# Row maxima from half-array matmuls in batches of four banks, in a two-layer encoder on one NeuronCore

## The chip, the core and the metric

The kernel runs on one core of one Trainium2 chip. A core has a matrix engine (TensorE, in the profile PE for its matmuls and PEld for its weight loads), a vector engine (DVE), a scalar engine (ACT), a general engine (POOL), an engine that only issues transfers (SP), and 16 DMA engines. Matmul results land in PSUM, which has eight banks of 128 partitions by 512 float32 numbers; everything else lies in SBUF. The engines run side by side, each working through its own list of instructions in order, and wait for each other through semaphores. The metric is the device time of one execution in microseconds (us), as the median of several runs.

## The reference

Two layers; in each, a normalised input is projected, one group of columns goes through a gated mixer and another through attention, and an output projection follows. The change touches attention alone:

```python
def gqa_axial_attention(q, k, v, qn_g, kn_g, tables):
    q = rmsnorm(q.reshape(b, s, H_B, HEAD_DIM), qn_g)
    k = rmsnorm(k.reshape(b, s, KV_HEADS, HEAD_DIM), kn_g)
    q = apply_axial_rope(q, tables)
    k = apply_axial_rope(k, tables)
    ...
    def attend(qblk):
        sc = jnp.einsum('bqkgd,bskd->bkgqs', qblk, k).astype(jnp.float32) * scale
        p = jax.nn.softmax(sc, axis=-1).astype(v.dtype)
        return jnp.einsum('bkgqs,bskd->bqkgd', p, v)
...
    y = jnp.concatenate([y_a, y_b], axis=-1)
    out = jnp.einsum('bse,ed->bsd', y, w_out[l])
    x = x + rmsnorm(out, post_g[l])
```

There are 2048 tokens, 8 query heads that share 2 key/value heads, and a head size of 64. A softmax needs a number near the largest score of each query row, which is subtracted before the exponential so that nothing overflows; any number near it gives the same softmax.

## The kernel before, in words

**Precision.** The operands are kept as two float16 parts, a high half and a low half. A product of two such operands takes three matmul passes.

**Layers and phases.** Each layer runs a projection phase (`Project.run`, matmul groups `pp`) and then an attention phase (`attend`). Work that isn't on the main line of a phase is hung into it at fixed places: `Background` (`bg`) runs jobs at ticks of the projection, one tick each 8 matmuls of 256 columns or each 4 of 512; in attention, `at(k, f)` hangs a job `f` at key tile `k`.

**Units and key tiles.** A unit is one tile of 128 tokens with one key/value head, four query heads wide, so there are 32 units in a layer. A unit goes over 16 key tiles (`NT`), and the main loop of `attend` counts key tiles of all units: `k = 16 u + n`, 512 in a layer. At each key tile PE makes a score bank `sp` with two matmuls of 512 columns, ACT reads it twice (`p_hi`, the exponential in float16, and `p_f`, the same in float32), and POOL or DVE makes the low half of it, `p_lo = p_f - p_hi`. Three key tiles later (`LAG`) PE takes twelve short matmuls of these against the values, into the bank `po`, which lives through the unit.

**Row maxima.** The maximum of a row must be known before its unit begins, so maxima are worked out ahead: for a unit, 4 heads times 4 groups of 512 keys make 16 steps. One step (`max_step`) is a matmul of 512 columns into a bank `pmax` and a reduction of it by DVE into a column of `mx`. The weights are `q_m`, in which partitions 0 to 63 hold the high half of the queries and 64 to 127 the low half, and `k_st` holds the high half of the keys twice, one copy in each half of the partitions. So a full-array matmul over 128 partitions gives high plus low half of the queries against the high half of the keys. The first 7 units (`PRE`) of a layer have their maxima in the projection phase, one step at each tick; the other 25 in the attention phase, spread evenly over its key tiles (`span`), 0.78 of a step at each. After the 16 steps `max_row` and `stack_max` (a transpose `t2` and two short rows) put the negated maxima into memory, from where the unit loads them as a part of `q2`.

**Filling work.** The output projection of a tile (48 matmuls `pout` of 512 columns, `out_steps`) is put into the list `fill`; at each key tile `pop_fill` takes some of them, spread evenly up to the key tile `fill_to` by `weight(k)`.

**End of a unit.** `gate` and `mul` (`finish`) read the bank `po` two key tiles after the last products; `turn_at` then transposes the tile's result (`py`), and `more` adds its output products to `fill`.

**What sets the order.** In attention all engines keep the program's order (`Pinned`). Within a key tile PE has: the two `sp` matmuls; the jobs hung there, `pmax` among them; the output products; and the twelve `po` matmuls of the key tile three back. All of `sp`, `pmax`, `pout`, `po`, `py`, `t2`, `pp` share the eight PSUM banks (`ps_t`). A new one takes the bank that was freed earliest in the program, and its first matmul waits until that bank's last reader is through.

**Who subtracts.** `dve_share(k)` gives 15 of 100 key tiles' `p_lo` to DVE and the others to POOL.

The helper `Pinned` records its engine's calls at line 89, so most instructions of attention carry the label L89 in the profile and are told apart by the names of their tiles.

Of the kernel before, what the change touches and what calls it, by code (L numbers as in the profile page):

```python
# [14 lines left out]
ALU = mybir.AluOpType  # L15
# [28 lines left out]
def encoder(ctx: ExitStack, tc, x, w_in, w_out, pre_g, post_g, ln_a_g, ln_a_b,  # L44
# [31 lines left out]
    def ps_t(name):  # L76
        return psum.tile([P, GRP], F32, name=name, tag="ps", bufs=8)
# [818 lines left out]
    Q_DELAY = 16  # L896
    PRE = 7
    PRE_WAIT = 19
    SHARE_0 = 15
    SHARE = 15  # L900
    T_DELAY = 9
    VA_DELAY = 13
    LAG = 3
# [8 lines left out]
    def attend(l, kv, nxt):  # L912
# [27 lines left out]
        def at(k, f):  # L940
            later.setdefault(k, []).append(f)
# [4 lines left out]
        def load_hl(dst, u):  # L946
            t, kv = units[u]
            for a in range(2):
                nc.sync.dma_start(dst[a * HD:(a + 1) * HD], q_d[t // TPG][kv, a, t % TPG])

        def load_qm(u):
            s = state[u]
            s.qm = f_t("q_m", dt=F16)
            load_hl(s.qm, u)
            s.mx = small.tile([P, NQ, NG], F32, name="mx", bufs=3)

        def load_q(u):
# [5 lines left out]
            nc.sync.dma_start(s.q2[0:HD], q_d[t // TPG][kv, 0, t % TPG])  # L963
            nc.sync.dma_start(s.q2[HD:HD + 2], m_d[t][kv])

        def max_step(u, n, pe, dve):
            s = state[u]
            j, c = n // NG, n % NG
            kv = units[u][1]
            ps = ps_t("pmax")  # L970
            pe.matmul(ps, s.qm[:, j * P:(j + 1) * P], k_st[:, kv, c * GRP:(c + 1) * GRP], start=True, stop=True)
            dve.tensor_reduce(s.mx[:, j, c:c + 1], ps, AX.X, ALU.max)  # L972

        def max_row(u, dve):
            s = state[u]
            s.m = small.tile([P, NQ], F32, name="m_neg", bufs=3)
            dve.tensor_reduce(s.m, s.mx, AX.X, ALU.max, negate=True)
# [248 lines left out]

        pre = min(PRE, len(units) - 2)
        steps = NQ * NG
        span = ((len(units) - 1) * NT - 16) // (len(units) - pre)

        def before():

            n0 = 0
            for u in range(pre):
                bg.add(n0 - 10 + PRE_WAIT, lambda u=u: load_qm(u))
                for n in range(steps):
                    bg.add(n0 + 4 + n + PRE_WAIT, lambda u=u, n=n: max_step(u, n, PE, nc.vector))
                bg.add(n0 + steps + 6 + PRE_WAIT, lambda u=u: max_row(u, nc.vector))
                bg.add(n0 + steps + 10 + PRE_WAIT, lambda u=u: stack_max(u, PE, nc.scalar, nc.vector))
                n0 += steps  # L1240
            bg.add(n0 + 4 + PRE_WAIT, lambda: load_q(0))
            bg.add(n0 + 4 + PRE_WAIT, lambda: load_qm(pre))
# [29 lines left out]
        for u in range(1, len(units)):  # L1272
            at(u * NT - 10, lambda u=u: load_q(u))
        for u in range(pre, len(units)):
            k0 = (u - pre) * span
            if k0 >= 8:
                at(k0 - 8, lambda u=u: load_qm(u))
            for n in range(steps):
                at(k0 + n * span // steps, lambda u=u, n=n: max_step(u, n, PE, DVE))
            at(k0 + span + 1, lambda u=u: max_row(u, DVE))  # L1280
            at(k0 + span + 5, lambda u=u: stack_max(u, PE, ACT, DVE))

        def load_gb(t):
            tiles[t].gb = f_t("gb")
# [2 lines left out]
        def pop_fill(n):  # L1287
            for _ in range(n):
                if fill:
                    fill.pop(0)()  # L1290

        def weight(k):
            return 2 if k >= total - 2 * NT else 1

        end = total + LAG
# [3 lines left out]

        def dve_share(k):  # L1300

            n = SHARE_0 if k < NH * NT else SHARE
            return k * n // 100 != (k + 1) * n // 100

        W_EARLY = total - 5 * NT
        gb_pieces = []
# [25 lines left out]
        def turn_at(k, t, cs):  # L1332
            trans, split = turn_steps(t, cs)
            at(k, trans)
            at(k + 1, split)
# [8 lines left out]
        for k in range(end):  # L1344
            if k < total:
                u, i = k // NT, k % NT
                s = state[u]
                kv = units[u][1]
                if i == 0 and kv == 0:
                    load_gb(units[u][0])  # L1350
                ss = slice(i * P, (i + 1) * P)
                sp = ps_t("sp")
                PE.matmul(sp, k_st[:, kv, ss], s.qs, start=True, stop=False)
                PE.matmul(sp, k_lo[0:HD + 2, kv, ss], s.q2[0:HD + 2], start=False, stop=True)
                ACT.activation(p_hi(k), sp, AF.Exp)
                ACT.activation(p_f(k), sp, AF.Exp)
                if not dve_share(k):
                    sub_lo(k, POOL)
            if post_queue:
                post_queue.pop(0)()  # L1360
            kb = k - 1
            if 0 <= kb < total and dve_share(kb):
                sub_lo(kb, DVE)
            for f in later.pop(k, []):
                f()
            if fill:
                room = sum(weight(q) for q in range(k, max(k + 1, fill_to)))
                pop_fill(-(-len(fill) * weight(k) // room))
            kb = k - LAG
            if 0 <= kb < total:  # L1370
                u, i = kb // NT, kb % NT
                s = state[u]
                kv = units[u][1]
                if i == 0:
                    s.av = ps_t("po")[:, 0:NQ * (HD + 1)].rearrange("p (t e) -> p t e", e=HD + 1)
                v_hi, v_lo = v16[:, i, kv, HD:VN], v16[:, i, kv, 0:HD]
                for j in range(NQ):
                    lhs = p_hi(kb)[:, j * P:(j + 1) * P]
                    PE.matmul(s.av[:, j], lhs, v_hi, start=i == 0 and j == 0, stop=False, skip_group_check=True)
                    PE.matmul(s.av[:, j, 0:HD], lhs, v_lo, start=False, stop=False, skip_group_check=True)  # L1380
                for j in range(NQ):
                    lhs = p_lo(kb)[:, j * P:(j + 1) * P]
                    PE.matmul(s.av[:, j], lhs, v_hi, start=False, stop=i == NT - 1, skip_group_check=True)
                if i == NT - 1:
                    t = units[u][0]
                    gate, mul = finish(u)
                    if u + 1 == len(units):
                        break
                    at(k + 1, gate)
                    at(k + 2, mul)  # L1390
                    if t == NT - 1:
                        turn_at(k + 6, t, (0, 1))
                        if nxt is None:
                            at(end - 1, lambda: last.extend(last_first()))
                        else:
                            more(k + 8, last_first, end)
                    elif kv == 1:
                        turn_at(k + 6, t, range(4))
                        if t in held:
                            more(k + 8, lambda t=t: held_steps(t), end)  # L1400
                        else:
                            more(k + 8, lambda t=t: out_steps(t), min(k + 8 + 2 * NT, end))
        assert not later
        gate()
        mul()
# [136 lines left out]
```

## Time and profile before

| | |
|---|---|
| runs | 2459.73, 2459.85, 2460.52 us; median 2459.85 us |
| the profiled execution | 2460.9 us, of which its span (first to last instruction) 2459.1 us |
| granted TensorE clock in it | 0.997 |
| attention of layer 0 and of layer 1 | about 554 to 1237 us and 1766 to 2440 us |
| matmuls `pmax` | 1024 (224 in the projections, 800 in attention) |

The profile gives for each engine its busy time, and in its timeline the start of each instruction with its length. A matmul's length there is its passage through the array with a modelled end, and the next one starts before it is over; what a matmul takes of PE's time is the distance from its start to the next start.

### The profile page before, as it was taken

The numbers are of one execution on the slowest core, as the hardware profiler recorded it, in microseconds if no ns is written. First come the engines' busy times: TensorE is split into PE (matmuls) and PEld (weight loads), VectorE is DVE, ScalarE is ACT, GpSimd is POOL, SyncE is SP. The second block draws the span as 40 slices with busy tenths as digits, with TensorE's granted clock in tenths as the row PEclk, the third lists the DMA queues.
The fourth block names the chain that finished last, engine by engine and source line by source line (L and its number), as shares of the span: only waits on it lengthen the run. The fifth ranks groups of instructions, "written<-read, shape, count | busy, mean of one in ns | idle before, by whom it ended". The sixth has DMA issues, their size and how long they took to land. (4 is left out here: it accounts for less than half of the span.)

```text
span 2459.1 us, 62836 instructions
## 1 busy us (share of the span) xinstructions
PE 2415.6 (98%) x25327; PEld 1600.6 (65%) x25327; DVE 1743.1 (71%) x4001; ACT 1638.0 (67%) x3545; POOL 1190.1 (48%) x1000
## 2 busy tenths in 40 slices
PE   7999999999999999999999999999999999999997
PEld 6988776445666666666589987754456666666664
DVE  7678556867777777777676875688667767777774
ACT  6565223148888888888854742231688888888886
POOL 2210110037777777777721111100577777777776
PEclk9999999999999999999999999999999999999999
DMA  6352222222121212121243422221321111212120
GB/s 199 121 178 72 66 62 64 67 88 73 51 81 52 67 51 70 60 64 49 83 166 113 152 60 71 73 73 43 110 63 38 57 54 43 68 43 68 51 68 27
DMA packets 174916, 188.11 MB, mean 76 GB/s; under 512 B 19608, under 2 KB 143648, under 8 KB 174624
## 3 DMA queue, kind: packets, MB, share of 16 engines
q1 hardware_dynamic: 174192, 182.52, 24.5%
q8 instruction: 198, 3.24, 0.6%
q10 hardware_dynamic: 432, 1.57, 0.2%
q14 instruction: 94, 0.77, 0.1%
HBM read 129.38 MB, written 54.66 MB: 75 GB/s over the span
## 5 line engine op out<-in xcount | busy, mean ns | idle before, releaser
L89 POOL TENSOR_TENSOR p_parts<-p_f,p_parts 128x512 f16<-128x512 f32 x872 | 1032.6, 1195 | 334.3 <-ACT p_f L89 253.9
L89 ACT ACTIVATE p_parts<-sp 128x512 f16<-128x512 f32 x1024 | 619.3, 605 | 175.1 <-PE sp L89 126.5
L89 PEld LDWEIGHTS <-p_parts 128*128 128x128 f16 x12288 | 510.0, 97 | 250.4 <-POOL p_parts L89 6.2
L89 DVE TENSOR_REDUCE mx<-pmax 128x1 f32<-128x512 f32 x800 | 541.4, 683 | 177.5 <-PE pmax L89 174.2
L89 PE MATMUL pp<-w_hl,hT 128*128 128x256 f16 x5376 | 619.3, 274 | 3.6 <-ACT w_hl L89 3.4
L89 ACT ACTIVATE p_f<-sp 128x512 f32<-128x512 f32 x1024 | 617.7, 603 | 0.0
L89 PEld LDWEIGHTS <-hT 128*128 128x128 f16 x5376 | 526.1, 98 | 70.8 <-issue 3.4
L89 PE MATMUL po<-v_st,p_parts 128*128 128x65 f16 (+1 forms) x12288 | 542.7, 193 | 7.0 <-POOL p_parts L89 4.5
L89 PE MATMUL pout<-wo,y_t 128*128 128x512 f16 x1536 | 488.2, 378 | 1.9 <-ACT y_t L89 1.7
L89 PE MATMUL sp<-q,k_t 66*128 66x512 f16 x1024 | 390.5, 381 | 0.0
L89 PE MATMUL sp<-q_st,k_t 128*128 128x512 f16 x1024 | 388.3, 379 | 1.6 <-DVE o_tok L89 1.3
L89 PE MATMUL pmax<-k_t,q_m 128*128 128x512 f16 x1024 | 387.1, 379 | 0.5 <-DVE hT L89 0.3
L89 PE MATMUL pp<-hT,w_hl 128*128 128x512 f16 x1536 | 370.3, 379 | 0.0
L89 PEld LDWEIGHTS <-y_t 128*128 128x128 f16 x1536 | 148.8, 97 | 177.8 <-ACT y_t L89 3.4
L89 PEld LDWEIGHTS <-w_hl 128*128 128x128 f16 x1536 | 149.6, 98 | 174.0
L89 PEld LDWEIGHTS <-q_m 128*128 128x128 f16 x1024 | 101.1, 99 | 120.9 <-issue 0.3
L972 DVE TENSOR_REDUCE mx<-pmax 128x1 f32<-128x512 f32 x224 | 150.2, 685 | 37.1 <-PE pmax L89 36.9
L89 POOL TENSOR_TENSOR wo<-wo_raw,wo 128x512 f16<-128x512 f32 x32 | 37.0, 1157 | 264.3 <-PE pp L89 223.0
L89 DVE TENSOR_TENSOR p_parts<-p_f,p_parts 128x512 f16<-128x512 f32 x152 | 118.0, 776 | 37.4 <-ACT p_f L89 36.6
L629 POOL TENSOR_TENSOR fl<-fv,fh 128x512 f16<-128x512 f32 x32 | 37.9, 1203 | 209.0 <-ACT fh L628 200.3
L89 PEld LDWEIGHTS <-k_t 128*128 128x128 f16 (+1 forms) x2048 | 131.3, 98 | 3.8 <-DVE o_tok L89 1.4
L547 ACT ACTIVATE fc<-pp,rs_y 128x64 f32<-128x64 f32 x320 | 69.7, 355 | 71.6 <-DVE rs_y L124 71.6
(212 smaller groups left out, 2042.9 us busy)
## 6 DMA issues: line engine op xcount, KB each, us to landing
w_raw<-in_w_in_dram SPq DMA_DIRECT2D x20, 512.0 KB
w_raw<-in_w_in_dram SPq DMA_DIRECT2D x10, 1024.0 KB
gb_d<-fa SPq DMA_DIRECT2D x32, 256.0 KB
wo_row<-in_w_out_dram SPq DMA_DIRECT2D x16, 512.0 KB
wo_raw<-in_w_out_dram SPq DMA_DIRECT2D x16, 512.0 KB
z_d<-fb SPq DMA_DIRECT2D x32, 256.0 KB
fb<-z_d SPq DMA_DIRECT2D x32, 256.0 KB
ya_d<-fa SPq DMA_DIRECT2D x32, 256.0 KB
```

Of the source, the lines that this page charges most:

```text
L89: return tc.keep_in_program_order(call(*args, **kw))
L547: nc.scalar.activation(qn[:, t, h], src[:, t, h], AF.Copy, scale=rs[:, i, t, h:h + 1])
L629: nc.gpsimd.tensor_tensor(s.lo, vh, s.hi, ALU.subtract)
L972: dve.tensor_reduce(s.mx[:, j, c:c + 1], ps, AX.X, ALU.max)
```

## The change

Four things are changed in how row maxima are made and placed.

- `load_qm` loads the high half of the queries into both halves of `q_m`'s partitions (two transfers of the same size as before). The low half of the queries no longer enters the row maximum, so this number differs slightly from before.
- `max_step` becomes `max_batch`: one head at a time, its four key groups together. Four banks are taken, four matmuls follow, each over 64 partitions, alternately the lower and the upper half, and then four reductions by DVE. In the projection phase a batch stands at each fourth tick.
- In attention the batches stand at the key tiles 0, 5, 8 and 13 of a unit (`BATCH`, from key tile 5 of the phase and up to 22 before the last unit), 100 of them, evenly picked from these. `weight(k)` is 0 there, so no output products are taken in these key tiles.
- `dve_share` is now the key tiles 1 and 10 of each unit, 2 of 16. `mul` comes one key tile earlier, the transposes of a finished tile two later, its output products one later. The last tile keeps its places.

```diff
-    SHARE_0 = 15
-    SHARE = 15
+    SHARE = (1, 10)
+    BATCH = (0, 5, 8, 13)
+    BATCH_FIRST = 5
...
             s.qm = f_t("q_m", dt=F16)
-            load_hl(s.qm, u)
+            t, kv = units[u]
+            for a in range(2):
+                nc.sync.dma_start(s.qm[a * HD:(a + 1) * HD], q_d[t // TPG][kv, 0, t % TPG])
...
-        def max_step(u, n, pe, dve):
+        def max_batch(u, j, pe, dve):
             s = state[u]
-            j, c = n // NG, n % NG
             kv = units[u][1]
-            ps = ps_t("pmax")
-            pe.matmul(ps, s.qm[:, j * P:(j + 1) * P], k_st[:, kv, c * GRP:(c + 1) * GRP], start=True, stop=True)
-            dve.tensor_reduce(s.mx[:, j, c:c + 1], ps, AX.X, ALU.max)
+            pm = [ps_t("pmax") for _ in range(NG)]
+            for c in range(NG):
+                r = slice(c % 2 * HD, c % 2 * HD + HD)
+                pe.matmul(pm[c], s.qm[r, j * P:(j + 1) * P], k_st[r, kv, c * GRP:(c + 1) * GRP],
+                          start=True, stop=True)
+            for c in range(NG):
+                dve.tensor_reduce(s.mx[:, j, c:c + 1], pm[c], AX.X, ALU.max)
...
-        span = ((len(units) - 1) * NT - 16) // (len(units) - pre)
+        slots = [u * NT + n for u in range(len(units) - 1) for n in BATCH]
+        slots = [k for k in slots if BATCH_FIRST <= k < (len(units) - 1) * NT - 22]
+        wanted = (len(units) - pre) * NQ
+        assert len(slots) >= wanted
+        slots = [slots[n * len(slots) // wanted] for n in range(wanted)]
...
-                for n in range(steps):
-                    bg.add(n0 + 4 + n + PRE_WAIT, lambda u=u, n=n: max_step(u, n, PE, nc.vector))
+                for j in range(NQ):
+                    bg.add(n0 + 4 + NG * j + PRE_WAIT, lambda u=u, j=j: max_batch(u, j, PE, nc.vector))
...
-            for n in range(steps):
-                at(k0 + n * span // steps, lambda u=u, n=n: max_step(u, n, PE, DVE))
-            at(k0 + span + 1, lambda u=u: max_row(u, DVE))
-            at(k0 + span + 5, lambda u=u: stack_max(u, PE, ACT, DVE))
+            own = slots[(u - pre) * NQ:(u - pre + 1) * NQ]
+            if u > pre:
+                at(own[0] - 8, lambda u=u: load_qm(u))
+            for j, k in enumerate(own):
+                at(k, lambda u=u, j=j: max_batch(u, j, PE, DVE))
+            at(own[-1] + 2, lambda u=u: max_row(u, DVE))
+            at(own[-1] + 6, lambda u=u: stack_max(u, PE, ACT, DVE))
...
         def weight(k):
+            if k in slots:
+                return 0
             return 2 if k >= total - 2 * NT else 1
...
-            n = SHARE_0 if k < NH * NT else SHARE
-            return k * n // 100 != (k + 1) * n // 100
+            return k % NT in SHARE
...
-                    at(k + 2, mul)
+                    at(k + 1, mul)
...
-                        turn_at(k + 6, t, range(4))
+                        turn_at(k + 8, t, range(4))
```

How the order moves is shown at two places. The first is PE in the attention of layer 1: one key tile with a row maximum before, and one with a batch now. `LDWEIGHTS` is a weight load and names what is loaded; `q_31935` is the tile `q2`; a bracket names the engines whose semaphore the instruction waits for. Before:

```order
40239 L89 LDWEIGHTS k_t
40240 L89 MATMUL sp<-q_st,k_t 128x512 [waits DVE_49]
40241 L89 LDWEIGHTS k_t
40242 L89 MATMUL sp<-q_31935,k_t 128x512
40243 L89 LDWEIGHTS q_m [waits DMAHW1_49,DMAHW0_49]
40244 L89 MATMUL pmax<-k_t,q_m 128x512 [waits Activation_49]
40245 L89 LDWEIGHTS y_t
40246 L89 MATMUL pout<-wo,y_t 128x512
40247 L89 LDWEIGHTS p_parts
40248 L89 MATMUL po<-v_st,p_parts 128x65
```

Now:

```order
40366 L89 LDWEIGHTS k_t
40367 L89 MATMUL sp<-q_31935,k_t 128x512
40368 L89 LDWEIGHTS q_m
40369 L89 MATMUL pmax<-k_t,q_m 128x512 [waits DVE_49]
40370 L89 LDWEIGHTS q_m
40371 L89 MATMUL pmax<-k_t,q_m 128x512 [waits Activation_49]
40372 L89 LDWEIGHTS q_m
40373 L89 MATMUL pmax<-k_t,q_m 128x512 [waits DVE_49]
40374 L89 LDWEIGHTS q_m
40375 L89 MATMUL pmax<-k_t,q_m 128x512 [waits DVE_49]
```

Four `pmax` stand together where one stood with an output product; each waits for the reader of the bank that it takes over, DVE or ACT, and the twelve `po` matmuls and the next key tile's `sp` are queued behind them.

The second place is DVE in the attention of layer 0, around the end of a unit (`rden`, `gb` and `o_tok` are `gate` and `mul`). Before:

```order
1376 L89 TENSOR_REDUCE mx<-pmax 128x1 [waits PE_49]
1377 L89 TENSOR_SCALAR rden<-po,cols 128x4 [waits PE_49]
1378 L89 RECIPROCAL rden<-rden 128x4 [waits DVE_49]
1379 L89 TENSOR_TENSOR gb<-gb,rden 128x2x2x64 [waits DVE_49]
1380 L89 TENSOR_REDUCE mx<-pmax 128x1 [waits PE_49]
1381 L89 TENSOR_TENSOR o_tok<-po,gb 128x2x2x64 [waits DVE_49]
1382 L89 TENSOR_REDUCE mx<-pmax 128x1 [waits PE_49]
1383 L89 TENSOR_TENSOR p_parts<-p_f,p_parts 128x512 [waits Activation_49]
1384 L89 TENSOR_REDUCE mx<-pmax 128x1 [waits PE_49] x3
```

Now:

```order
1126 L89 TENSOR_TENSOR p_parts<-p_f,p_parts 128x512 [waits Activation_49]
1127 L89 TENSOR_REDUCE m_neg<-mx 128x4 [waits DVE_49]
1128 L89 TENSOR_SCALAR rden<-po,cols 128x4 [waits PE_49]
1129 L89 RECIPROCAL rden<-rden 128x4 [waits DVE_49]
1130 L89 TENSOR_TENSOR gb<-gb,rden 128x2x2x64 [waits DVE_49]
1131 L89 TENSOR_TENSOR o_tok<-po,gb 128x2x2x64 [waits DVE_49]
1132 L89 TENSOR_REDUCE mx<-pmax 128x1 [waits PE_49] x4
1133 L89 SCALAR_TENSOR_TENSOR m_rows<-t_12903,m_rows 4x128 [waits DMAHW2_49,Activation_49]
1134 L89 TENSOR_REDUCE mx<-pmax 128x1 [waits PE_49] x4
1135 L89 TENSOR_TENSOR o_t<-pout,g_post 128x512 [waits Activation_49]
```

The reductions stood singly between other work; now they come in fours, one batch right behind `gate` and `mul`, the next with hardly anything of DVE's between.

More of the change, by code (lines that the diff above doesn't have):

```diff
@@ L1274, in attend @@
         for u in range(pre, len(units)):
-            k0 = (u - pre) * span
-            if k0 >= 8:
-                at(k0 - 8, lambda u=u: load_qm(u))
-            for n in range(steps):
-                at(k0 + n * span // steps, lambda u=u, n=n: max_step(u, n, PE, DVE))
-            at(k0 + span + 1, lambda u=u: max_row(u, DVE))
-            at(k0 + span + 5, lambda u=u: stack_max(u, PE, ACT, DVE))
+            own = slots[(u - pre) * NQ:(u - pre + 1) * NQ]
[5 more added lines that the diff above has]
+            at(own[-1] + 6, lambda u=u: stack_max(u, PE, ACT, DVE))
         def load_gb(t):
@@ L1367, in attend @@
                 room = sum(weight(q) for q in range(k, max(k + 1, fill_to)))
-                pop_fill(-(-len(fill) * weight(k) // room))
+                pop_fill(-(-len(fill) * weight(k) // max(room, 1)))
             kb = k - LAG
@@ L1397, in attend @@
                     elif kv == 1:
-                        turn_at(k + 6, t, range(4))
+                        turn_at(k + 8, t, range(4))
                         if t in held:
-                            more(k + 8, lambda t=t: held_steps(t), end)
+                            more(k + 9, lambda t=t: held_steps(t), end)
                         else:
-                            more(k + 8, lambda t=t: out_steps(t), min(k + 8 + 2 * NT, end))
+                            more(k + 9, lambda t=t: out_steps(t), min(k + 9 + 2 * NT, end))
         assert not later
```

## The prediction

> **What bounds the kernel now.** I read the page's busy times and its forty slices first, then the stretches of the two attention phases and of the projection stretch in which row maxima run, then what PE waited for.
>
> ```profile
> PE 2415.6 (98%) x25327; PEld 1600.6 (65%) x25327; DVE 1743.1 (71%) x4001; ACT 1638.0 (67%) x3545; POOL 1190.1 (48%) x1000
> PE   7999999999999999999999999999999999999997
> PEclk9999999999999999999999999999999999999999
> 554.00:1237.00 683.00, 675.98 (x8446) 412.51 (x8444) 511.95 (x1000) 594.64 (x1195) 519.61 (x436) 1.00 0.21 66
> 1766.00:2440.00 674.00, 669.76 (x8403) 407.73 (x8401) 464.60 (x867) 580.93 (x1147) 512.73 (x436) 1.00 0.18 54
> 430.00:554.00 124.00, 124.00 (x585) 57.13 (x584) 91.53 (x165) 39.15 (x79) 18.51 (x16) 1.00 0.26 77
> PE po L89 <- POOL p_parts L89: 4.5, 6, 1.3
> PE pmax L89 <- DVE mx L89: 0.2, 1, 0.2
> ```
>
> The three rows of stretches give length, then busy time of PE, PEld, DVE, ACT and POOL, then the granted clock and DMA. PE has no gap worth the name: 676 of 683 us in the first attention, 670 of 674 in the second, all of the 124 us of projection in which `pmax` runs, at full clock. It waits 4.5 us in all for POOL's low halves and 0.2 us for a reduction of `pmax`. But a busy PE is a row of overlapping modelled ends, so the price of a matmul is read from starts, in a piece of the timeline of attention (start, length, engine):
>
> ```profile
> 899.45 2.01 DVE L89 TENSOR_REDUCE mx<-pmax 128x1 f32<-128x512 f32 x3
> 899.91 0.38 PE L89 MATMUL sp<-q_st,k_t 128*128 128x512 f16 x1
> 900.13 0.38 PE L89 MATMUL sp<-q,k_t 66*128 66x512 f16 x1
> 900.13 0.10 PEld L89 LDWEIGHTS <-q_m 128*128 128x128 f16 x1
> 900.35 0.38 PE L89 MATMUL pmax<-k_t,q_m 128*128 128x512 f16 x1
> 900.57 0.38 PE L89 MATMUL pout<-wo,y_t 128*128 128x512 f16 x1
> 900.78 0.53 PE L89 MATMUL po<-v_st,p_parts 128*128 128x65 f16 x12
> 901.15 0.38 PE L89 MATMUL sp<-q_st,k_t 128*128 128x512 f16 x1
> 900.55 0.60 ACT L89 ACTIVATE p_parts<-sp 128x512 f16<-128x512 f32 x1
> 901.04 0.59 ACT L89 ACTIVATE p_f<-sp 128x512 f32<-128x512 f32 x1
> ```
>
> Each matmul of 512 columns starts 0.22 us after the one before (899.91 to 900.78 is 0.87 us for four), though each row says 0.38; the twelve `po` take 0.37. So PE is full of starts, and **time taken from or given to PE in these phases is time of the kernel**, as long as nobody else becomes late. All `pmax` cost 1024 x 0.2175 = 223 us of starts.
>
> **The change, part by part.** *The matmuls.* Four full-array steps took 0.87 us. Now they are two pairs, each of a lower and an upper half of the array's rows. No row before shows two row halves at work. The nearest rows are matmuls that alternate between two halves of the array's columns, in the projection at 251 us:
>
> ```profile
> 250.96 0.71 PE L89 MATMUL pp<-w_hl,hT 128*128 128x256 f16 x5
> 251.60 0.30 PE L89 MATMUL pt<-ws,fh 128*64 128x128 f16 x4
> 251.74 0.22 PE L89 MATMUL pt<-ws,fl 128*64 128x128 f16 x2
> 251.79 0.28 PE L89 MATMUL pt<-ws,fh 128*64 128x128 f16 x4
> 251.91 0.22 PE L89 MATMUL pt<-ws,fl 128*64 128x128 f16 x2
> 251.96 0.28 PE L89 MATMUL pt<-ws,fh 128*64 128x128 f16 x4
> 252.07 0.22 PE L89 MATMUL pt<-ws,fl 128*64 128x128 f16 x2
> 252.13 0.28 PE L89 MATMUL pt<-ws,fh 128*64 128x128 f16 x4
> 252.24 0.22 PE L89 MATMUL pt<-ws,fl 128*64 128x128 f16 x2
> 252.40 0.39 PE L89 MATMUL pp<-w_hl,hT 128*128 128x256 f16 x2
> 251.60 0.14 PEld L89 LDWEIGHTS <-fh 128*64 128x64 f16 x4 [0.21 <-issue]
> 240.71 0.38 PE L89 MATMUL pt<-v_row,ones 1*128 1x1 f32 x2 [0.37 <-DVE v_row L683]
> 241.02 0.28 PE L89 MATMUL pp<-w_hl,hT 128*128 128x256 f16 x1
> L89 PE MATMUL pt<-v_row,ones 1*128 1x1 f32 x4 | 0.8, 256 | 0.7 <-DVE v_row L683 0.7
> ```
>
> Two things are to be seen. **A pair runs side by side**: from 251.74 to 252.24 the rows repeat each 0.166 us, six matmuls of 128 columns, so a pair takes 0.055, what one alone would (a full matmul of 512 columns takes 0.2175, a quarter of it 0.054). **Going over and back costs**: from the first of the five `pp` at 250.96 to the `pp` at 252.40 are 1.44 us; five times 0.109 (half of 0.2175) and twelve pairs of 0.055 make 1.21, which leaves 0.23 us, and the weight loads, which elsewhere start beside the matmul ahead (900.13), sat idle for 0.21 us until 251.60. For row halves I take the same price, since it is the nearest whole block; below it would be nothing, above it the rivals. The one matmul on a single row (240.71) speaks for some price on rows too: the second of its two, 256 ns long on the mean, ends at 241.09 and so starts at about 240.84, and the next `pp` comes 0.18 later, for one column.
>
> So a batch costs 2 x 0.2175 + 0.225 = 0.66 us in place of 0.87: **0.21 us less, in 256 batches (200 in attention, 56 in the projections) 53.8 us less.** With no price for going over it would be 256 x 0.435 = 111 us less.
>
> The Trainium skill, "TensorE: Matmul & The Clock Gate", section "Part 3: Packing small matmuls", says that a weight load goes beside a running matmul only where the row group differs. By that, the third and fourth load of a batch, which go into a half that is still at work, would be laid bare. The trace of before disagrees for the whole array: the load of `q_m` at 900.13 begins with the matmul in flight on the same rows. I follow the trace, and keep the rule as a rival.
>
> *The reductions.* Their number stays at 1024. They are to be hidden beside PE, as now:
>
> ```profile
> L89 DVE TENSOR_REDUCE mx<-pmax 128x1 f32<-128x512 f32 x800 | 541.4, 683 | 177.5 <-PE pmax L89 174.2
> L89 POOL TENSOR_TENSOR p_parts<-p_f,p_parts 128x512 f16<-128x512 f32 x872 | 1032.6, 1195 | 334.3 <-ACT p_f L89 253.9
> L89 DVE TENSOR_TENSOR p_parts<-p_f,p_parts 128x512 f16<-128x512 f32 x152 | 118.0, 776 | 37.4 <-ACT p_f L89 36.6
> L89 ACT ACTIVATE p_parts<-sp 128x512 f16<-128x512 f32 x1024 | 619.3, 605 | 175.1 <-PE sp L89 126.5
> 554.00:1237.00 683.00, 151.64 (x400) 270.04 (x400) 1.00 0.21 66
> ```
>
> Three in a row take 2.01 us (899.45), so four 2.7 us. During these, four of eight banks are held, a fifth by `po`, and `sp` and `pout` have the rest. What the four `pmax` wait for is seen in the order: readers of older banks on DVE or ACT; behind them on PE stand twelve `po` and the next `sp`, for which ACT, and then POOL, wait. Whether DVE is through in time: besides `mx` (270 us, the last row, which is `pmax` alone) it has 512 - 270 = 242 us in 512 key tiles of layer 0, 0.47 each. After the change a key tile takes (683 - 21) / 512 = 1.29 us. Between key tiles 5 and 8 there are 3.9 us for 2.7 + 3 x 0.47 = 4.1 us of DVE, between 0 and 5 there are 6.5 for 5.1. So DVE just fails on the short distance and recovers on the long one; since only work ahead of the reductions delays them, I put the cost between nothing and 0.21 us a batch, and take 0.055 us, **14 us in all**, a quarter of the way up, because over eight key tiles DVE has room (9.2 of 10.3 us). In the projection stretch DVE has 91.5 of 124 us busy, much the same share.
>
> *Placing.* Output products are the same number in fewer key tiles; PE's list is as long. A key tile without batch has 0.87 of `sp` and two products and 0.37 of `po`, 1.24 us; ACT's two passes go through in 1.0 us (900.55 to 901.04 is 0.49 from start to start; the 605 ns of its row overlap as PE's do), so PE stays the later one. *Shares:* 24 subtractions go from DVE (24 x 0.776 = 19 us less) to POOL (24 x 1.195 = 29 us more, 14 in a phase of which it has 520 of 683 busy): nothing on PE's path; were POOL late, `po` would wait, 4.5 us in all now. *Loads of q_m:* two transfers as before. *`mul` earlier, transposes later:* frees the bank of `po` sooner, and the last tile keeps its places; nothing.
>
> Sum: 2460.9 (the profiled execution: span 2459.1 and 1.8 around it) - 53.8 + 14 = 2421.1; the median of the runs lies 1.05 below that execution, so **2420 us**.
>
> **The rivals.**
> *Going over is cheap on rows.* For it: nothing shows its price on row halves, and a load of 64 rows keeps its 128 columns. Against it: the block at 251.6 and the single row at 241. With 0.05 us in place of 0.225 it is 45 us less: 2375.
> *Banks come late.* DVE's fours hold half of PSUM, and the short distance is 0.2 us short. For it: the 4.1 against 3.9. Against it: PE hardly waited for DVE so far, and DVE's total falls. At 0.21 us a batch the gain is gone: 2445 to 2470.
> *The halves take turns.* If two row halves can't run together, a batch costs 4 x 0.2175 + 0.225 = 1.10 us, 0.225 more in 256 batches, 58 us: 2517, slower. It decides as soon as the second of a pair starts later than about 0.1 us after the first: then a pair saves less than its share of the 0.225. For it: a pair of row halves writes two banks at once, twice what the column pairs wrote. Against it: the pairs at 251.7. The Trainium skill, "TensorE: Matmul & The Clock Gate", section "Measured speedup vs the span model", gives 3.07x for four row tiles of 512 columns, which speaks against this rival; no run here shows it yet.
> *Loads laid bare.* By a load of 0.10 us (900.13) in each batch, 26 us of the gain go: 2446. This is what the skill's rule above would give.
> *It doesn't do what it says.* If the 64-row matmuls run as full-array ones, four starts of 0.2175 stay and nothing is switched; with the waits of the fours it is 2459 to 2470.
>
> **How the numbers follow.** Forecast 62% (2400 to 2440), cheap 12%, banks late 10%, taking turns 8%, loads bare 5%, not as it says 3%. About 0.2%, 5 us, is what a measurement of this kernel can tell from no change. Faster: 62 + 12 + 5 and half of the late banks, 84%; same: the other kernel in disguise and a part of the late banks, 6%; slower 10%. The range goes from 2378 to 2458: left out are the cheapest part of the second case, the case of turns and the worst of the late banks, about 20%.
>
> **What would show it.** In the timeline of a batch the second `pmax` starts some hundredths of a us after the first, the third 0.22 after that; from the last `sp` to the first `po` of the key tile 0.9 us (0.22 and 0.66), not 1.1 or 1.3. Weight loads of `q_m` behind an idle stretch of PEld show the price of going over; its size decides between the first two cases. PE's waits for DVE `mx` and for ACT's `p_f` should sum to 5 to 25 us; above 50 the banks decide. The mean length of a key tile in attention should be 1.29 us. I am wrong if the pairs start 0.2 us apart, or if PE's waits in key tiles 0, 5, 8, 13 eat what the pairs save.

## The result, and the profile after

The changed kernel takes **2432.89 us** (median of 4 runs, 2430.52 to 2434.02), the kernel before beside it 2460.18 us: a ratio of 0.9886 (95% interval 0.987 to 0.9901), 27.3 us less. The forecast was 2420. The profiled execution took 2433.87 us, its span 2432.1.

From the page of the changed kernel, the busy times and two groups (busy time, mean ns of one | idle time before them):

```profile
PE 2373.2 (98%) x25327; PEld 1512.5 (62%) x25327; DVE 1725.5 (71%) x3977; ACT 1637.0 (67%) x3545; POOL 1235.0 (51%) x1024
L89 DVE TENSOR_REDUCE mx<-pmax 128x1 f32<-128x512 f32 x800 | 496.0, 682 | 153.4 <-PE pmax L89 152.8
L89 PE MATMUL pmax<-k_t,q_m 64*128 64x512 f16 x1024 | 164.3, 382 | 6.2 <-DVE o_tok L89 3.6
```

The two attention phases as windows (length, then busy time of PE, PEld, DVE, ACT, POOL, then granted clock and DMA):

```profile
549.50:1229.00 679.50, 665.03 (x8448) 380.11 (x8447) 507.41 (x988) 594.12 (x1196) 542.38 (x448) 0.99 0.21 66
1755.40:2413.90 658.50, 649.41 (x8401) 372.29 (x8400) 461.13 (x855) 580.89 (x1147) 535.13 (x448) 1.00 0.18 56
```

And what PE waited for, the entries that were not there before or have grown (total, times, longest):

```profile
PE pout L89 <- ACT y_t L89: 4.0, 3, 1.8
PE pmax L89 <- DVE o_tok L89: 3.6, 7, 0.7
PE sp L89 <- DVE o_tok L89: 2.9, 1, 2.9
PE t L89 <- DVE mx L89: 2.5, 6, 0.4
PE sp L89 <- DVE mx L89: 1.3, 1, 1.3
```

Of these, the kernel before had, with more than half a us,

```profile
PE pout L89 <- ACT y_t L89: 1.7, 3, 0.6
PE sp L89 <- DVE o_tok L89: 1.3, 1, 1.3
```

Attention of layer 1 went from 674 to 658.5 us, that of layer 0 only from 683 to 679.5. PE is still busy 98% of the span, but its waits for DVE and ACT are more and longer.

**What a batch costs**, in the timeline of the changed kernel (start, length, engine):

```profile
2001.69 0.38 PE L89 MATMUL sp<-q_st,k_t 128*128 128x512 f16 x1
2001.90 0.38 PE L89 MATMUL sp<-q,k_t 66*128 66x512 f16 x1
2002.21 0.11 PEld L89 LDWEIGHTS <-q_m 64*128 64x128 f16 x4 [0.43 <-issue]
2002.22 0.61 PE L89 MATMUL pmax<-k_t,q_m 64*128 64x512 f16 x4
...
2002.76 0.54 PE L89 MATMUL po<-v_st,p_parts 128*128 128x65 f16 x12
```

Four matmuls of 512 columns have ended (by the modelled end) 0.61 us after the first began. Their single starts, which the row puts together, lie 0.003, 0.223 and 0.003 us apart (medians over the batches). From the last `sp` to the first `pmax` it is 0.313, from the last `pmax` to `po` 0.308; without a change of layout both are 0.22. So a switch costs 0.095 us going over and 0.09 going back. From the last `sp` to `po` the median is 0.851 us; with four full-array `pmax` (e1_full below) it is 1.084, as in

```profile
2017.00 0.38 PE L89 MATMUL sp<-q,k_t 66*128 66x512 f16 x1
2017.22 1.03 PE L89 MATMUL pmax<-k_t,q_m 128*128 128x512 f16 x4
```

with the first `po` at 2018.08. **The halves save 0.233 us in each of 256 batches, 60 us, more than forecast; 33 of these are missing in the time.**

**Where they went**, in the same timeline, around the end of a unit (three dots stand for rows left out):

```profile
1902.39 1.71 DVE L89 SCALAR_TENSOR_TENSOR o_t<-o_t,rs_o,x_r 128x512 f32<-128x512 f32 x1
1902.40 5.58 POOL L89 TENSOR_TENSOR p_parts<-p_f,p_parts 128x512 f16<-128x512 f32 x4 [1.37 <-ACT p_f L89]
...
1904.49 0.92 DVE L89 TENSOR_TENSOR gb<-gb,rden 128x256 f32<-128x256 f32 x1
...
1904.83 0.60 PE L89 MATMUL pmax<-k_t,q_m 64*128 64x512 f16 x3
...
1905.44 0.42 DVE L89 TENSOR_TENSOR o_tok<-po,gb 128x256 f32<-128x256 f32 x1
1905.78 1.18 DVE L89 SCALAR_TENSOR_TENSOR o_t<-o_t,rs_o,x_r 128x512 f32<-128x512 f32 x1
...
1905.92 0.39 PE L89 MATMUL pmax<-k_t,q_m 64*128 64x512 f16 x1 [0.49 <-DVE o_tok L89]
...
1906.89 2.47 DVE L89 TENSOR_REDUCE mx<-pmax 128x1 f32<-128x512 f32 x4
...
1907.62 0.27 PE L89 MATMUL t<-ident,m_neg 128*4 128x128 f32 x1 [0.41 <-DVE mx L89]
```

The fourth `pmax` takes over the bank of the unit's old `po`, which DVE gives up only when `o_tok` has been made from it; then `o_t` stands ahead of the reductions on DVE, and a transpose waits for them. By the starts of its matmuls PE loses 1.4 us there (0.86 at the fourth `pmax`, with a second pair that is torn apart, and 0.57 at the transpose), at key tile 5 of three units in each layer. DVE's `o_t` takes 1.71 us beside POOL's subtraction and 0.74 without one (the row at 1172.30 below). The largest single wait is of the same kind, with more of DVE's work ahead of it. DVE's rows of the changed kernel's timeline there:

```profile
1167.69 1.37 DVE L89 SCALAR_TENSOR_TENSOR w_hl<-w_big,w_col,w_hl 128x256 f16<-128x256 f32 x1
1168.99 1.64 DVE L89 SCALAR_TENSOR_TENSOR o_t<-o_t,rs_o,x_r 128x512 f32<-128x512 f32 x1
...
1171.96 0.42 DVE L89 TENSOR_TENSOR o_tok<-po,gb 128x256 f32<-128x256 f32 x1
1172.30 0.74 DVE L89 SCALAR_TENSOR_TENSOR o_t<-o_t,rs_o,x_r 128x512 f32<-128x512 f32 x1
```

PE's rows at the same place:

```profile
1172.44 0.61 PE L89 MATMUL sp<-q_st,k_t 128*128 128x512 f16 x1 [2.87 <-DVE o_tok L89]
1172.84 0.63 PE L89 MATMUL sp<-q,k_t 66*128 66x512 f16 x1
```

And the window behind them, with the columns of the windows above:

```profile
1172.50:1177.50 5.00, 5.00 (x33) 2.59 (x34) 4.97 (x13) 2.17 (x4) 1.62 (x2) 0.50 0.66 184
```

PE waits 2.87 us, and then its matmuls start 0.4 us apart, for 5 us: the window's granted clock is 0.50. In the trace the clock is halved from 1171.5 to 1178.3, and the wait ended at 1172.4; half of the 5.9 us from there on, 2.9 us, is an estimate of what this costs, so this wait is paid twice. The traces of e1, e4, e5 and e10 below have a wait of 2.4 to 2.9 us at this place and a stretch of 3.4 or 6.8 us at half the clock beside it; those of e9, e11 and e12, where the wait is 0.5 to 0.7 us, have no such stretch there. Ahead of its last 10 us the clock is halved for 20.4 us of the changed kernel's trace, at four places, and for 6.8 of the kernel before: at half speed that is some 7 us of the 33 (an estimate), most of which is in the sum below too. Not all four places follow a wait of this kind: one is at 24.6 us, where the two kernels do the same.

To sum it up I take, for each two neighbouring matmuls, what their starts lie further apart than is usual for that pair, where it is over 0.02 us. In the two attention phases together:

| kernel | lost by PE, us |
|---|---|
| before | 17.7 |
| changed | 38.6 |
| e1_full (full-array batches) | 22.8 |
| e4_turn6 | 33.3 |
| e11_stt34 | 26.0 |
| e12_stt34full (e11, full-array batches) | 19.8 |

That is 21 us more after the change than before; by the same sum the projection phases lose 18.7 in place of 13.8, 5 us more. So 26 of the 33 are found; some 7 remain that the sum doesn't place. The sum hangs on which pairs are taken together for what is usual. Taken by tile and shape, with the four `pmax` of a batch kept apart, it gives 17.1 before and 42.7 after in attention, and 25.4 and 31.6 in the rest: 32 us more, with the six kernels in the same order. So the 7 us may be no more than a matter of the method.

### The profile page after: what moved, and what is told of

Read it like the earlier page. It is cut to its first block, busy times and chain, and to the rows that moved or that the text cites. A ratio compares the mean times of both kernels' runs of the same rounds, so it can differ in the third digit from the quotient of the medians.

```text
span 2432.1 us, 62853 instructions
## 1 busy us (share of the span) xinstructions
PE 2373.2 (98%) x25327; PEld 1512.5 (62%) x25327; DVE 1725.5 (71%) x3977; ACT 1637.0 (67%) x3545; POOL 1235.0 (51%) x1024
## 5 line engine op out<-in xcount | busy, mean ns | idle before, releaser
L89 POOL TENSOR_TENSOR p_parts<-p_f,p_parts 128x512 f16<-128x512 f32 x896 | 1077.5, 1216 | 270.0 <-ACT p_f L89 217.6
L89 PEld LDWEIGHTS <-p_parts 128*128 128x128 f16 x12288 | 495.1, 97 | 291.1 <-issue 91.0
L89 DVE TENSOR_REDUCE mx<-pmax 128x1 f32<-128x512 f32 x800 | 496.0, 682 | 153.4 <-PE pmax L89 152.8
L89 PE MATMUL pout<-wo,y_t 128*128 128x512 f16 x1536 | 463.2, 379 | 5.1 <-ACT y_t L89 4.0
L89 PE MATMUL pp<-hT,w_hl 128*128 128x512 f16 x1536 | 347.5, 379 | 1.0 <-DVE mx L978 1.0
L89 PE MATMUL pmax<-k_t,q_m 64*128 64x512 f16 x1024 | 164.3, 382 | 6.2 <-DVE o_tok L89 3.6
L978 DVE TENSOR_REDUCE mx<-pmax 128x1 f32<-128x512 f32 x224 | 140.4, 682 | 29.2 <-PE pmax L89 28.9
L89 DVE TENSOR_TENSOR p_parts<-p_f,p_parts 128x512 f16<-128x512 f32 x128 | 91.8, 717 | 53.8 <-ACT p_f L89 50.1
L658 ACT ACTIVATE pp<-fa 128x512 f32<-128x512 f32 x32 | 19.2, 600 | 146.5 <-DVE fa L657 146.5
```

The costliest lines, as they stand in the source:

```text
L89: return tc.keep_in_program_order(call(*args, **kw))
L658: nc.scalar.activation(pg, th, AF.Square, accum_out=self.ysq[:, g, c:c + 1])
L978: dve.tensor_reduce(s.mx[:, j, c:c + 1], pm[c], AX.X, ALU.max)
```

## The experiments

All medians stand beside runs of the kernel before on the same chip (2458.4 to 2460.9 us). As these differ by 2.5 us from chip to chip, a difference of 3 us between two experiments is not much.

**e1_full**: batches over the whole array, with the high and low halves of the queries again; all else as changed.

```diff
-            for a in range(2):
-                nc.sync.dma_start(s.qm[a * HD:(a + 1) * HD], q_d[t // TPG][kv, 0, t % TPG])
+            load_hl(s.qm, u)
...
-                r = slice(c % 2 * HD, c % 2 * HD + HD)
+                r = slice(0, P)
```

> The changed kernel with the matmuls of a batch over all 128 partitions again (high and low half of the queries, loads as before the change), everything else as changed: batches, places, no output products there. Theory (the gain is the row halves: a batch took 0.63 us from the last score matmul's end to the first product, in place of 0.87): about 0.24 us x 256 = 61 us slower than the changed kernel, 2480 to 2494 us, above the kernel before by what the fours cost in waits (20 to 33 us). Rival (the gain is the new placing, not the halves): within 5 us of the changed kernel, 2428 to 2438.

Measured 2466.83 us (2462.09 to 2470.43), ratio 1.0029 [1.0018, 1.004]. Neither number came. The halves are worth 34 us, not 60; and the rest of the change (batches, placing, shares, transposes) alone costs 7 us. PE loses 22.8 us in attention here, 5 us more than before and 16 less than with the halves. So fours of banks are hardly slow in themselves: most of the waits come up when PE gets through a batch sooner.

**e2_pairs**: one pair at each even key tile instead of two at one of four, so twice as many switches.

```diff
-    BATCH = (0, 5, 8, 13)
+    BATCH = (0, 2, 4, 6, 8, 10, 12, 14)
...
-            pm = [ps_t("pmax") for _ in range(NG)]
-            for c in range(NG):
+            j, b = divmod(j, 2)
+            pm = {c: ps_t("pmax") for c in (2 * b, 2 * b + 1)}
+            for c in pm:
...
```

(Left out are the same change at the reductions and the places of the 512 smaller batches.)

> Row halves, but batches of two banks at the even key tiles, so one pair at a time: the same 1024 matmuls, 512 switches in place of 256. Theory (0.19 us for going over and back, 0.22 for a pair; two banks cause hardly a wait): 0.41 us for a pair against 0.435 for two full matmuls, 512 x 0.025 = 13 us less than before, with waits of 0 to 10 us: 2447 to 2457. Rival (the switch costs little and the fours' waits are what was lost): below the changed kernel, 2395 to 2420.

2468.0 us (2464.91 to 2471.54), ratio 1.0034 [1.0023, 1.0045]: slower than either theory said. Its timeline gives the price again (start, length):

```profile
2000.54 0.38 PE L89 MATMUL sp<-q,k_t 66*128 66x512 f16 x1
2000.85 0.39 PE L89 MATMUL pmax<-k_t,q_m 64*128 64x512 f16 x2
2001.17 0.54 PE L89 MATMUL po<-v_st,p_parts 128*128 128x65 f16 x12
```

0.63 us from `sp` to `po` (median 0.635), less 0.22: 0.415 for a pair, against 0.435 for two full matmuls. By starts the pairs should still have won some 10 us (512 times 0.02); they lost 8. I can't fully place these 18: the rest of the change, which cost 7 us in e1, is in e2 too, and by the sum above PE loses 7 us more in attention than in the kernel before. That is less than half.

**e3_late6**: the batch of key tile 5 one later, away from `o_tok`.

```diff
-    BATCH = (0, 5, 8, 13)
+    BATCH = (0, 6, 9, 13)
```

> The changed kernel with the batches at key tiles 0, 6, 9 and 13 in place of 0, 5, 8 and 13. Theory (the lost time is mostly the batch at key tile 5, whose bank is freed by the end of the unit's multiply on DVE; key tiles 5 and 6 took 0.19 us too long in layer 1 and 0.45 in layer 0, over some 29 units, 18 us): 10 to 18 us less than the changed kernel, 2415 to 2423. Rival (any batch three key tiles behind another waits, wherever it stands; 6 to 9 and 13 to 0 are three): no change, 2428 to 2438.

2432.68 us (2432.61 to 2434.01), ratio 0.9892 [0.9877, 0.9907]: nothing, as the rival said. PE's waits of `pmax` for `o_tok` fell from 3.6 to 2.0 us, but waits for `o_t` took their place, 3.6 us where 0.8 had been.

**e4_turn6**: the transposes of a finished tile where they stood before.

```diff
-                        turn_at(k + 8, t, range(4))
+                        turn_at(k + 6, t, range(4))
```

> The changed kernel with the transposes of a finished tile at their old place, two key tiles earlier. Theory (the first output products of tile 14 in each layer wait 1.9 us for the split of these transposes, 0.8 us before the change; nothing else hangs on it): 2 us less, 2429 to 2433. Rival (the earlier transposes take a bank and DVE time between the batches at key tiles 5 and 8): 3 to 8 us more, 2436 to 2441.

2426.82 us (2425.26 to 2431.26), ratio 0.987 [0.9855, 0.9885], 6 us below the changed kernel; the runs of the two just overlap. The changed kernel put the transposes two key tiles later and the products that need them only one, and a held tile's products meet the gap; its timeline has

```profile
1200.37 0.38 PE L89 MATMUL sp<-q,k_t 66*128 66x512 f16 x1
...
1201.82 0.62 ACT L89 CAST y_t<-py 128x512 f16<-128x512 f32 x1
...
1202.50 0.60 PE L89 MATMUL pout<-wo,y_t 128*128 128x512 f16 x2 [1.75 <-ACT y_t L89]
```

Of the 4.0 us that `pout` waits for ACT's `y_t`, 0.5 are left in e4 (and 1.2 more for DVE's part of it). The span is 8.6 us shorter, but much of that is not the edit's. Ahead of the last 10 us the clock is halved for 10.2 us in this trace and for 20.4 in the changed kernel's, which makes some 5 us (an estimate). Up to 600 us, ahead of the first transposes, where the two kernels are the same, it is 3.4 against 10.2, so that some 3 of the 5 us can't be the edit's. Waiting 1.5 us less for `k_t` in the second projection need not belong to it either. The single runs agree: at a granted clock of 0.997 e4 took 2425.26 and 2425.31 us, at 0.994 it took 2428.32 and 2431.26, beside 2430.52 to 2434.02 at 0.994 and 0.995 in the changed kernel. At a like clock the edit is worth some 3 us, about what the theory said.

**e5_fill** and **e6_share15**: output products in all key tiles again; and DVE's share as before the change.

```diff
-            if k in slots:
-                return 0
```

> The changed kernel with one part undone: output products are again spread over all key tiles, those with a batch included. Theory: PE's list is as long as before, and what PE waits for is a DVE chain (row sums' reciprocal, gate, product) that ends after the last po of a unit, so where the output products stand hardly matters: 2429 to 2437 us, PE's wait of pmax for o_tok still 2.5 us or more. Rival: key tiles with a batch need more work of PE to cover DVE's four reductions, as four full-array starts did: 2417 to 2427, and the waits of pmax for DVE below 1.5 us.

2433.91 us (2432.1 to 2434.47), ratio 0.9895 [0.9879, 0.9912]: no difference, as the theory said. (Its wait of `pmax` for `o_tok` is gone all the same; PE waits 6.7 us for `o_t` at `sp` instead.)

```diff
-            return k % NT in SHARE
+            return k * 15 // 100 != (k + 1) * 15 // 100
```

> The changed kernel with the shares undone: DVE subtracts the low halves in 15 of 100 key tiles again, at places that move from unit to unit, not in key tiles 1 and 10. Theory: 24 subtractions more on DVE (24 x 0.72 = 17 us of 1725) and 24 fewer on POOL are not on PE's path; but some now fall beside a batch or ahead of the product that frees the bank of po, where DVE is late: 2434 to 2442. Rival: POOL is what slows DVE (o_t took 1.7 us beside a subtraction on POOL, 0.74 without), so fewer of them on POOL help: 2422 to 2430.

2433.92 us (2432.59 to 2435.75), ratio 0.9898 [0.9883, 0.9913]: 1 us above the changed kernel, no difference that can be told, just below the theory's band and not the rival's. How many subtractions DVE makes hardly matters; e9 asks where.

**e7_shift**: e4 with batches clear of the unit's end.

```diff
-    BATCH = (0, 5, 8, 13)
+    BATCH = (2, 7, 11, 15)
```

> The kernel of e4_turn6 with the batches in key tiles 2, 7, 11 and 15 instead of 0, 5, 8 and 13. Theory: the wait at key tile 5 is for the bank of the unit's old po, which is free only when DVE's chain behind the last po is through (about 1.9 us after it, in key tile 5); from key tile 7 on no batch meets it, so the six waits of 1.2 us in attention and PE's wait of pmax for o_tok (3.6 us) go: 2415 to 2422. Rival: DVE is late for its total work wherever the batches stand, as when key tile 5 was moved to 6: 2424 to 2431.

2440.31 us (2438.66 to 2444.03), ratio 0.9926 [0.9911, 0.9941]: some 14 us worse than e4, so the theory falls, and the rival's band is passed too. Its wait for `o_tok` did go; but PE's waits now have

```profile
PE pout L89 <- DVE o_t L89: 6.6, 23, 0.6
...
PE sp L89 <- DVE o_t L89: 5.5, 12, 0.5
```

The bank was only where DVE's lateness showed. Moved, it shows elsewhere, and more of it: by the second way of taking the sum of starts PE loses 54.1 us in attention here and 39.4 in e4.

**e8_evac**: e4 with `po` copied by ACT to SBUF, so that its bank is free at once.

```diff
+            def free():
+                out = small.tile([P, NQ, HD + 1], F32, name="av_sb", bufs=2)
+                ACT.copy(out, s.av)
+                s.av = out
...
+                    at(k + 1, free)
                     at(k + 1, gate)
...
```

> The kernel of e4_turn6 with one copy on ACT more in each unit: po is copied out of its bank as soon as its last key tile is done, and DVE's chain reads the copy. Theory: as in e7, the bank of po is what the batch in key tile 5 waits for: the copy frees it 1.5 us sooner, the wait of pmax for o_tok goes, and ACT's 62 copies of about 0.4 us are hidden in part: 2419 to 2425. Rival: ACT is the next to be late (two exponentials in 1.0 of 1.27 us), so 62 copies on it cost more than the bank gives: 2428 to 2440.

2523.64 us (2517.45 to 2524.87), ratio 1.0257 [1.0242, 1.0273]: 97 us worse than e4, far beyond both. PE waits for DVE, and DVE's `rden` in turn for ACT's copy:

```profile
PE sp L89 <- DVE mx L89: 55.9, 42, 4.0
...
  ACT av_sb L89: 63.7, 42
```

So the rival has a part in it. On the mean of the units, from the last `po` on, DVE's chain ends 2.5 us later than in e4: it begins 1.0 us later, behind the copy, and takes 1.5 us longer, 3.4 and not 1.9. The granted clock is lower too, 0.986 to 0.989 in these runs. Why the chain takes longer is seen in three of its operations, by tile (shortest/median/longest, ns), in e8:

```profile
L89 DVE TENSOR_TENSOR gb<-gb,rden x64: 424/1262/1364, 576.6 to 2504.0; 128x256 f32<-128x256 f32 x64
L89 DVE TENSOR_TENSOR o_tok<-av_sb,gb x62: 425/1264/1360, 577.1 to 2491.1; 128x256 f32<-128x256 f32 x62
L89 DVE TENSOR_TENSOR o_tok<-po,gb x2: 424/424/425, 1271.6 to 2504.5; 128x256 f32<-128x256 f32 x2
...
L89 DVE TENSOR_SCALAR rden<-av_sb,cols x62: 229/954/1237, 575.4 to 2488.4; 128x4 f32<-128x4 f32 x62
L89 DVE TENSOR_SCALAR rden<-po,cols x2: 222/222/222, 1270.6 to 2503.6; 128x4 f32<-128x4 f32 x2
```

and in the changed kernel:

```profile
L89 DVE TENSOR_TENSOR gb<-gb,rden x64: 425/930/1336, 576.5 to 2414.6; 128x256 f32<-128x256 f32 x64
L89 DVE TENSOR_TENSOR o_tok<-po,gb x64: 424/424/426, 577.6 to 2415.1; 128x256 f32<-128x256 f32 x64
```

**This is the clue.** `o_tok` takes 424 to 426 ns in every one of 64 cases while one operand is in PSUM (`po`), and 1264 at the median once both are in SBUF (`av_sb`, `gb`). A product of 4 numbers a row went from 222 to 954 ns. Such an operation of DVE waits for the subtraction that POOL is at: in the changed kernel's trace 60 of the 64 `gb` start while POOL is at one, and each of these ends 279 to 284 ns after that subtraction does, however much of it was left (0.4 to 1.05 us); the other four take 425 to 427 ns. In e8 58 of the 62 `o_tok` start beside POOL, and end 279 to 287 ns after it. POOL is busy 80% of the time (542 of 679.5 us in the changed kernel's window above). The Trainium skill, "SBUF — State Buffer", section "Who interferes with whom", says that a DVE operation with two inputs in SBUF contends with a POOL operation that reads SBUF, since its second input comes through a shared port, and that this port is an exclusive lock; the lengths and the ends here agree.

**e9_share34**: e4, and DVE's two subtractions where POOL should then be still while DVE's chain runs.

```diff
-    SHARE = (1, 10)
+    SHARE = (3, 4)
```

> The kernel of e4_turn6 with DVE's two subtractions of a unit in key tiles 3 and 4 instead of 1 and 10: as many on DVE and on POOL as before, but POOL now stands still while DVE's chain behind the last po of a unit runs. Theory: DVE is late since its operations with two operands in SBUF are held up by a subtraction that runs on POOL (gb took 0.92 us at 1904.49 of the changed kernel, 0.42 where POOL is still), so the chain gets shorter and the waits in key tile 5 shrink: 2417 to 2423, most gb near 0.42. Rival: the two subtractions stand in DVE's queue just ahead of the batch's four reductions and take 1.4 us there, more than the chain gains: 2427 to 2436.

2423.8 us (2423.41 to 2425.94), ratio 0.9844 [0.9828, 0.9861], 3 us below e4, with intervals that overlap: just off the theory's band, and not the rival's. `gb` got shorter only in part (median 921 ns, mean 928 where e4 has 1003; the forecast of 424 was wrong); the sums of `o_t` went from 1105 to 954 ns on the mean. The trace shows why: 51 of the 64 `gb` still run beside a subtraction on POOL (62 in the changed kernel), but only 30 of the 56 such `o_t` (55 in the changed kernel).

**e10_stt**: e4, and the chain with an operand in PSUM throughout.

```diff
-                gv = heads(tl.gb)
-                rd = s.rd.rearrange("p (h k) -> p h k", h=2).unsqueeze(3)
-                DVE.tensor_tensor(gv, gv, rd.broadcast_to([P, 2, 2, HD]), ALU.mult)
...
-                av = s.av[:, :, 0:HD].rearrange("p (h k) e -> p h k e", h=2)
-                DVE.tensor_tensor(heads(tl.on), av, heads(tl.gb), ALU.mult)
+                for j in range(NQ):
+                    o = kv * NQ * HD + (j % 2 * 2 + j // 2) * HD
+                    DVE.scalar_tensor_tensor(tl.on[:, o:o + HD], s.av[:, j, 0:HD], s.rd[:, j:j + 1],
+                                             tl.gb[:, o:o + HD], ALU.mult, ALU.mult)
```

> The kernel of e4_turn6 with the chain behind the last po rebuilt: instead of gb times rden (both in SBUF) and then po times gb, four operations, one for each head, multiply po by rden and by gb at once, each with one operand in PSUM and one in SBUF. Theory: these aren't held up by POOL, so that rden, reciprocal and four of about 0.25 us free the bank of po 1.4 us after the last po and not 1.9: the waits of pmax for o_tok fall below 1.5 us in all, 2419 to 2424. Rival: PE's lost time sits elsewhere on DVE (the sums of o_t and x_r, the weights' splits), or four small operations take as long as the two: 2425 to 2431.

2425.38 us (2424.38 to 2426.46), ratio 0.9851 [0.9836, 0.9866]: 1.4 us below e4, which can't be told from nothing, and in the rival's band. PE's waits of `pmax` for `o_tok` fall to 0.2 us, as the theory said (the long one of `sp` stays, 2.4), but `o_t`, which has both operands in SBUF, comes next and is held up longer (mean 1287 ns, 1105 in e4), so that the gain is given back there.

**e11_stt34**: both.

> e9_share34 and e10_stt together. Theory: with the chain free of POOL by its operands, a still POOL in key tiles 3 and 4 brings little more, only shorter sums of o_t and x_r: 2416 to 2423, no more than 3 us below the better of the two. Rival: the two add up: 2410 to 2416.

**2417.92 us** (2417.02 to 2419.38), ratio 0.9821 [0.9807, 0.9836]: 9 us below e4, 15 below the changed kernel, and the best of all. This lies in the theory's band, but 6 us below the better of the two and not 3: by the ratios to the kernel before, e9 and e10 lie 0.0026 and 0.0019 below e4, and e11 0.0049. The two gains add up, as the rival said, if not to its band. The place shown above, now in e11:

```profile
1893.17 0.74 DVE L89 SCALAR_TENSOR_TENSOR o_t<-o_t,rs_o,x_r 128x512 f32<-128x512 f32 x1
...
1893.83 1.29 DVE L89 TENSOR_TENSOR p_parts<-p_f,p_parts 128x512 f16<-128x512 f32 x2
...
1893.89 0.61 PE L89 MATMUL pmax<-k_t,q_m 64*128 64x512 f16 x4
...
1895.03 2.48 DVE L89 TENSOR_REDUCE mx<-pmax 128x1 f32<-128x512 f32 x4
...
1895.78 0.27 PE L89 MATMUL t<-ident,m_neg 128*4 128x128 f32 x1 [0.37 <-DVE mx L89]
```

With POOL still, `o_t` takes 0.74 us and not 1.18; the four `pmax` are in one row, with no wait among them, and the reductions begin 1.1 us after the first of them, not 2.1.

**e12_stt34full**: e11 with the full array, as e1 is to the changed kernel (`load_hl` and `slice(0, P)`).

> The kernel of e11_stt34 with the halves undone, as in e1_full: batches of four full-array matmuls. Between e1_full and the changed kernel the halves were worth 34 us, while the starts of pmax and the two changes of layout give 60. Theory: the 26 us that are missing are DVE's lateness, which a longer batch on PE covers; so in a kernel where DVE's chain is short the halves are worth more, and the full array has less to gain from the short chain: 2458 to 2464, 40 to 46 us above e11_stt34. Rival: DVE's chain costs both kernels the same, and the halves are worth 34 us here too: 2450 to 2454.

2463.88 us (2459.93 to 2468.16), ratio 1.0015 [1.0005, 1.0025]: 46 us above e11, as the theory said. The same halves are worth 34 us where DVE is late and 46 where it is less so, and what helps the halves by 15 us helps the full array by 3. The granted clock explains a part of this at most: its mean is 0.9948 in the changed kernel's runs and 0.9966 in e1's, 0.9958 and 0.9959 in e11's and e12's. With the missing share of each run's span taken off its time, as an estimate, the halves are worth 38 and 46 us. That is the answer to where the gain went: **into waits for DVE that a slower PE had covered.**

## Why the prediction came out as it did

The mechanism was right, and so was the range; the sum was 13 us too low because one term was mis-sized by 19 us. That the sum was not 19 us off is luck: the batches saved 6 us more than forecast.

- *Pairs run side by side*: right. The second starts 0.003 us after the first, so the halves don't take turns.
- *The price of going over and back*, 0.225 us from column halves: 0.19 measured, a batch 0.63 in place of 0.66, and the term of 53.8 us is 60.
- *Loads laid bare*: not so. The four loads of a batch take 0.11 us together at 2002.21, so the third and fourth go in while the first pair is at work in the same halves. The rule that the prediction gives from the Trainium skill, "TensorE: Matmul & The Clock Gate", section "Part 3: Packing small matmuls", doesn't hold here as it stands; the section also lets a load into a background weight buffer go ahead, which the prediction left out.
- *The banks' waits*, 14 us: **this is the term that was mis-sized.** About 33 us of the gain are missing, of which 26 are seen as PE's waits and the stretches at half the clock. Over 256 batches the 33 us are 0.13 us each, between the forecast's 0.055 and the 0.21 of the rival *Banks come late*, which was thus about half right. Its form was wrong too: not an even cost in each batch, but 1.4 us at key tile 5 of a few units and single waits of up to 2.9 us. The step that failed is "242 us in 512 key tiles of layer 0, 0.47 each": a mean, and of lengths that aren't DVE's own. DVE's other work comes in clusters at a unit's end, and each of its operations on two SBUF operands may wait for POOL. The profile of before had shown it, shortest, median and longest of `gb`:

```profile
L89 DVE TENSOR_TENSOR gb<-gb,rden x64: 424/872/1437, 579.0 to 2440.6; 128x256 f32<-128x256 f32 x64
```

- *Placing* at nothing: right (e5). *Shares* at nothing: right for the number (e6), wrong for the places (e9, e11). *Transposes later* at nothing: wrong, by some 3 us at a like clock (e4). *`mul` earlier* at nothing: no run shows it alone.
- *What would show it*: the pairs and the idle PEld came as described. PE's waits for `mx` add up to 6.4 us (2.5, 1.3 and 0.6 in attention, 2.0 in the projections), within the 5 to 25; but I had named the wrong waits: `o_tok`, `o_t` and `y_t` make another 12. A key tile takes 1.31 us on the mean, not 1.29: 679.5 / 512 = 1.33 in layer 0, from which the 1.29 was worked out, and 658.5 / 512 = 1.29 in layer 1. In layer 0 DVE also splits the next layer's weights.

That halves save more where DVE is less late is shown by e1, e12 and the two kernels beside them. That DVE's operations are held up by POOL is shown by e8's lengths and by their ends, a fixed time behind POOL's, and is used in e9 to e11. Where the last 2 to 7 us went is open, and so is more than half of e2's loss. Some of the stretches at half the clock follow no long wait, and what set these off isn't shown.

## What to carry to other kernels

When an engine that is busy all the time is made faster, its gain is that of its starts only as far as the others' work at each place, in clusters and not on the mean, is through in time: look for operations of one shape with a wide spread between shortest and longest in the profile before, since something may hold these up, as POOL did here. It paid here to keep one operand of DVE's critical operations in PSUM and POOL still while the others ran (e11). A batch that crosses between layouts of the array should be long: here two pairs for each crossing took 0.63 us in place of 0.86, one pair 0.415 in place of 0.435.

## What the hardware showed that I had not expected

- DVE with both operands in SBUF beside a busy POOL: 1264 ns in place of 424, and 954 in place of 222 for four numbers a row (e8). With an operand in PSUM the same operation took 424 to 426 ns in every case of the two kernels. Held up, it ends some 280 ns after POOL's subtraction, whatever was left of that.
- Two 64-row matmuls of 512 columns side by side start 0.003 us apart, and the next pair 0.223 later: each half works at full speed. Changing from 128 to 64 rows costs 0.095 us, changing back 0.09.
- Beside a wait of 2.87 us PE's granted clock fell to 0.50, for 6.8 us in all, of which 5.9 lay behind the wait.
